# Sample heads as two planner streams ahead of the attention units, sparse keys prepared beside the last dense head

## The chip, the cores and the metric

One core of a Trainium2 chip. The time is device microseconds of one execution. The core has five engines that run their own instruction lists in order: TensorE (PE; its weight loads are shown as PEld), VectorE (DVE), ScalarE (ACT), GpSimd (POOL) and the sync engine (SP), which here issues all DMAs from one queue.

## What is computed

One layer of a hybrid attention encoder, for one new stream of 2048 frames (the prompt) and, beside it, 8 streams of 16 new frames each with 256 cached frames (the sample). One input projection feeds three groups of heads, and one output projection joins them:

```python
p = _split_proj(_rmsnorm(x, g), w_in, b_f)
oa = _forget_block(...)   # A: 8 heads, causal softmax attention with forget gates
ob = _dsa_block(...)      # B: 8 heads (2 of keys), attention over the best 256 keys of an indexer
oc = _band_prompt(...)    # C: 8 heads, own chunk and the 8 chunks before
y = x + concat(oa * silu(za), ob * silu(zb), oc * silu(zc)) @ w_out   # then RMSNorm
```

The sample goes through the same three kinds of heads (24 in all), with keys and values from the caches and from the new rows. Keys, values and queries are used as pairs of 16-bit halves, so every product is made of two or three matmuls.

## The kernel before

**A planner writes the order.** The kernel's Python is a set of generators, `Stream`s (line 163). Each yields a condition, a time by which its next inputs are due, and issues instructions when it is resumed. `drive` (line 436) keeps a clock of each engine by a table of costs (`Clock`, line 63) and resumes, again and again, the stream that is due: steps without TensorE go by their time, steps with TensorE go in the order in which the streams are handed to `drive`, the first that is due, and `slack` (line 48; 300 ns for the sample) holds a stream's matmuls back until their inputs are surely there. Gates (`gate`, `landed`, lines 423 to 430) open when something is planned to be done. All of it happens while the program is written: the engines see only their lists and semaphores. All instructions come from one helper, so the profile gives line 196 for all; they are told apart by their tiles.

**The stages.** After normalisation and gates, `load_stream` and `fill_stream` (lines 846, 855) run the input projection in groups of 256 columns (tiles `wt`, `hT`, `pj`, evacuated to `ev` and stored by DMA). The list `groups` (line 832) sets their sequence: pairs of A and C heads by `HO`, with five B groups between (keys and values, then four of queries and gates). The projection fills TensorE while the attention runs in `units` (`run`, line 1896): 16 dense heads (A and C) of 4 units each, then sparse blocks 15 down to 0 of 128 queries, 2 units each. A unit takes maxima of its scores (VectorE), scores (TensorE, tile `st`), exps (ScalarE, `Pf`), the low half (`Pl`, GpSimd or VectorE), and products (TensorE, `o`). `prep_stream` (line 1979) prepares each dense head: loads keys and values that the projection has stored (`kn`, `vn`), splits them (`khl`, `V`), turns the keys (`tr`, `Ka`, `K`). A head is prepared once the groups up to its own have landed. After the last dense head the same stream runs `b_prep`, the sparse heads' tables (`BTb`, `ng`) and keys and values (`KaB`, `VB`), when the projection is all done. `out_all` (line 1994) then runs the output projection (`wo`, `gac`) block by block; block 16, the sample's, opens when the sample is done.

**The sample** (`sample_stream`, line 1349; main loop from 1606) is one stream, started when the sparse selection is done. It has no memory of its own: it uses tiles that the selection leaves free. Loads of cached keys and values go to the halves of `rl`, split keys to `qi`, turned keys and the spread queries to `yy`, values and spread weights to `acc`, scores and weights to `cum`, bias to `eq`; its matmuls go through `pj`. Head after head, in this order: `keys`, bias, `softmax`, `products` of the head before, `values`. It stands behind the units in the list that is handed to `drive` (line 1941): select, load, products, rows, index scores, scores, maxima, preparation, sample, then the projection and the output projection as fillers.

Of the kernel before, what the change touches and what calls it, by code (L numbers as in the profile page):

```python
# [264 lines left out]
def hybrid_step(ctx, tc, x_prompt, x_sample, cache_a_k, cache_a_v, cache_a_logf, cache_b_k, cache_b_v,  # L265
# [1083 lines left out]
    def sample_stream():  # L1349
# [67 lines left out]

        def ahead(nm, src):

            def one(g0):  # L1420
                n = min(4, 17 - g0)
                t = row(nm)
                load(t, src, g0, n)
                return t

            nxt = [one(0), one(4)]
            for g0 in range(0, 17, 4):
                yield g0, min(4, 17 - g0), nxt.pop(0)
                if g0 + 8 < 17:
                    nxt.append(one(g0 + 8))  # L1430
# [175 lines left out]
        yield from gate_sums()  # L1606
        yield landed(grouped, last[sorder[0]])
        after = None
        order = [4 * g + r for g in sorder + [2, 3] for r in range(4)] + [0]
        for k, hg in enumerate(order[:-1]):  # L1610
            g, r = divmod(hg, 4)
            if hg == 8:
                if after is not None:
                    yield from after()
                    after = None
                yield from select_s()
                yield landed(grouped, last[2])
            if r == 0:
                qp4 = sl.tile([128, 4, 128], F16, name="qp4", bufs=1)
                q24 = sl.tile([128, 4, 128], F16, name="q24", bufs=1)  # L1620
                rows = [qTd[e, g * 256:(g + 1) * 256, SEQ:NT].rearrange("(h d) t -> d h t", d=64) for e in range(2)]
                SP.dma_start(qp4[0:64], rows[0])
                SP.dma_start(qp4[64:128], rows[0])
                SP.dma_start(q24[0:64], rows[1])
            if hg < 8:
                ks, vs, bias = parts(cak, sak, hg), parts(cav, sav, hg), gate_bias(hg)
            elif hg >= 16:
                ks, vs, bias = parts(cck, sck, hg - 16), parts(ccv, scv, hg - 16), rel_bias(hg - 8)
            else:
                ks, vs, bias = parts(cbk, sbk, g - 2), parts(cbv, sbv, g - 2), rel_bias(hg - 8)  # L1630
            new = hg < 8 or hg >= 16 or r == 0
            more, bias = bias, next(bias)
            if new:
                Ka = yield from keys(ks)
            yield from more
            hl = yield from softmax(qp4[:, r, :], q24[0:64, r, :], Ka, bias)
            if after is not None:
                yield from after()
                yield landed(grouped, last[order[k + 1] // 4])
            if r == 0:  # L1640
                SP.dma_start(sz4, szd[g * 4:(g + 1) * 4, 4, :, 0:64].rearrange("h p d -> p h d"))
            if new:
                yield from values(vs)

            def after(hl=hl, sz=sz4[:, r, :], gs=gs4, r=r, g=g):
                yield from products(*hl, sz, gs[:, r, :])
                if r == 3:
                    for e in range(2):
                        SP.dma_start(gTd[e, g * 256:(g + 1) * 256, SEQ:NT].rearrange("(h d) t -> d h t", d=64),
                                     gs[e * 64:(e + 1) * 64])  # L1650
        yield from after()
# [447 lines left out]
```

## Time and profile before

| | |
|---|---|
| median of 3 runs | 2649.38 us (2643.98 to 2650.48) |
| profiled execution | 2649.79 us, its span 2648.0 us |
| busy: PE / PEld | 2397.8 / 1674.7 us (91% / 63% of the span) |
| busy: DVE / ACT / POOL | 1802.8 / 1381.3 / 1100.3 us |
| DMA | 257.24 MB, mean 97 GB/s |
| mean granted TensorE clock | 0.973 of full speed |

The profile is one execution. The page cuts the span into 40 slices of 66.2 us and gives each engine's busy share in tenths; TensorE has 9 in nearly all of them, and less in the first, in four from 1655 us on (4, 7, 8, 8) and in the last (5). A waiting time is put down to what ended it. Busy time of TensorE is modelled, since matmuls overlap: the distance between the starts of two matmuls in a row says what one costs.

### The profile page before, as it was taken

The numbers are of one execution on the slowest core, as the hardware profiler recorded it, in microseconds if no ns is written. First come the engines' busy times: TensorE is split into PE (matmuls) and PEld (weight loads), VectorE is DVE, ScalarE is ACT, GpSimd is POOL, SyncE is SP. The second block draws the span as 40 slices with busy tenths as digits, with TensorE's granted clock in tenths as the row PEclk, the third lists the DMA queues.
The fourth block names the chain that finished last, engine by engine and source line by source line (L and its number), as shares of the span: only waits on it lengthen the run. The fifth ranks groups of instructions, "written<-read, shape, count | busy, mean of one in ns | idle before, by whom it ended". The sixth has DMA issues, their size and how long they took to land. (4 is left out here: it accounts for less than half of the span.)

```text
span 2648.0 us, 69046 instructions
## 1 busy us (share of the span) xinstructions
PE 2397.8 (91%) x26752; PEld 1674.7 (63%) x26838; DVE 1802.8 (68%) x4900; ACT 1381.3 (52%) x2734; POOL 1100.3 (42%) x1730
## 2 busy tenths in 40 slices
PE   4998999999999998999999999478899999999995
PEld 3666677766766776686776876355455555555543
DVE  6333778876787868778685566487866677778542
ACT  6324666766656774766744454365554444444110
POOL 0012556663443544534452043255665444544100
PEclk9999999999999999999999999689999999999997
DMA  6247323434343222233445433643533334334531
GB/s 192 60 92 198 92 67 80 107 96 99 94 94 106 71 76 76 72 103 83 120 99 124 120 76 81 135 94 67 144 83 86 79 83 106 84 86 108 127 99 26
DMA packets 553189, 257.24 MB, mean 97 GB/s; under 512 B 376064, under 2 KB 541760, under 8 KB 552592
## 3 DMA queue, kind: packets, MB, share of 16 engines
q1 hardware_dynamic: 552848, 252.71, 38.8%
q8 instruction: 212, 3.47, 0.6%
q14 instruction: 129, 1.06, 0.1%
HBM read 160.37 MB, written 84.85 MB: 93 GB/s over the span
## 5 line engine op out<-in xcount | busy, mean ns | idle before, releaser
L196 POOL TENSOR_TENSOR Pl<-Pf 128x512 f16<-128x512 f32 (+3 forms) x688 | 683.4, 1003 | 582.2 <-ACT Pf L196 544.6
L196 PE MATMUL pj<-wt,hT 128*128 128x128 f16 (+1 forms) x8568 | 779.2, 243 | 11.3 <-DVE ev L196 10.9
L196 PEld LDWEIGHTS <-hT 128*128 128x128 f16 x8976 | 653.2, 98 | 117.5 <-issue 22.0
L196 ACT ACTIVATE Pf<-st,sh 128x512 f32<-128x512 f32 (+1 forms) x496 | 297.9, 613 | 282.9 <-DVE st L196 111.1
L196 PEld LDWEIGHTS <-Pf 128*128 128x128 bf16 x5472 | 314.9, 98 | 104.2 <-issue 9.8
L196 PE MATMUL pj<-wo,gac 128*128 128x512 f16 x1224 | 290.5, 383 | 13.2 <-DMA gac<-gTd 11.6
L196 PE MATMUL pj<-hT,wt 128*128 128x512 f16 (+1 forms) x1440 | 293.6, 348 | 0.3 <-DVE ev L196 0.3
L196 PEld LDWEIGHTS <-Pl 128*128 128x128 f16 x2736 | 255.3, 99 | 18.5 <-POOL Pl L196 16.4
L196 DVE SCALAR_TENSOR_TENSOR acc<-rl,iws,acc 128x512 f32<-128x512 f32 (+3 forms) x266 | 196.2, 738 | 87.1 <-ACT rl L196 82.5
L196 DVE CUSTOM_DVE_ANT_0 jk<-s,ng 128x512 bf16<-128x512 f32 (+3 forms) x304 | 188.7, 621 | 84.6 <-PE s L196 67.4
L196 ACT ACTIVATE Pf<-st,ncb 128x512 f32<-128x512 f32 (+1 forms) x320 | 192.1, 623 | 92.8 <-PE st L196 80.3
L196 DVE TENSOR_REDUCE mx<-s 128x1 f32<-128x512 f32 (+2 forms) x320 | 185.0, 603 | 67.0 <-PE s L196 66.1
L196 ACT ACTIVATE rl<-s 128x512 f32<-128x512 f32 (+3 forms) x304 | 161.3, 544 | 110.8 <-PE s L196 55.7
L196 ACT ACTIVATE ev<-pj 128x512 f32<-128x512 f32 (+4 forms) x211 | 115.2, 546 | 194.0 <-PE pj L196 181.3
L196 PE MATMUL o<-V,Pf 128*128 128x65 f16 x3296 | 213.2, 194 | 1.0 <-ACT Pf L196 0.9
L196 PE MATMUL o<-V,Pl 128*128 128x65 f16 x1648 | 196.2, 193 | 13.3 <-POOL Pl L196 12.3
L196 PEld LDWEIGHTS <-wt 128*128 128x128 f16 x1440 | 126.3, 98 | 129.2 <-issue 13.9
L196 PEld LDWEIGHTS <-gac 128*128 128x128 f16 x1224 | 116.5, 98 | 139.5 <-DMA gac<-gTd 12.7
L196 PE MATMUL st<-qp,Ka 128*128 128x512 f16 (+3 forms) x544 | 180.9, 335 | 8.8 <-ACT Pf L196 8.7
L196 ACT ACTIVATE eq<-acc,us 128x384 bf16<-128x384 f32 (+13 forms) x126 | 165.4, 1313 | 39.6 <-POOL us L196 38.0
L196 PE MATMUL st<-Q,K 98*128 98x512 f16 (+3 forms) x544 | 182.2, 336 | 1.7 <-ACT Q L196 1.7
L196 PE MATMUL o<-VB,Pf 128*128 128x65 f16 (+1 forms) x2176 | 132.4, 194 | 3.6 <-DVE rq_t L196 1.9
(449 smaller groups left out, 4299.8 us busy)
## 6 DMA issues: line engine op xcount, KB each, us to landing
wst<-in_w_in SPq DMA_DIRECT2D x84, 256.0 KB
gac<-gTd SPq DMA_DIRECT2D x34, 384.0 KB
out<-ev SPq DMA_DIRECT2D x96, 128.0 KB
qTd<-ev SPq DMA_DIRECT2D x96, 128.0 KB
szd<-ev SPq DMA_DIRECT2D x96, 128.0 KB
qp<-qTd SPq DMA_DIRECT2D x96, 128.0 KB
out<-xr SPq DMA_DIRECT2D x17, 512.0 KB
xt<-in_x_prompt SPq DMA_DIRECT2D x16, 512.0 KB
```

Of the source, the lines that this page charges most:

```text
L196: r = f(*args, **kw)
```

## The change

Three things change; the arithmetic stays.

1. The last group of the projection is now the fourth group of B queries and gates, which only the sparse heads read. It stood before the last pairs of A heads. The marks that sparse heads wait for (`last[2]`, `last[3]`) move with it.
2. `b_prep` leaves `prep_stream` and becomes a stream of its own, with the same gate (projection done).
3. The sample becomes two streams. `first` makes keys, bias, scores and weights of head after head, `second` values, products and the output. Plain lists join them: `first` is at most one head ahead of `second`; `begin` asks for the first two tiles of the next head's keys or values as soon as the ones before are used. Both stand ahead of the units in the list for `drive`.

```diff
-        if 2 <= k < 7:
+        if 2 <= k < 6:
             groups += [(group_b, max(k - 3, 0), int(k > 2))]
-            last[2] = last[3] = len(groups)
...
+    groups += [(group_b, 3, 1)]
+    last[2] = last[3] = len(groups)
...
+        early = {}
         def ahead(nm, src):
...
-            nxt = [one(0), one(4)]
+            nxt = early.pop(nm, None) or [one(nm, src, 0), one(nm, src, 4)]
...
+        def begin(nm, src):
+            early[nm] = [one(nm, src, 0), one(nm, src, 4)]
...
+        def first():
+            yield from gate_sums()
+            yield upto(order[0])
+            for k, hg in enumerate(order):
+                g, r = divmod(hg, 4)
+                if hg == 8:
+                    yield gate(lambda: len(done) == k)
+                    yield from select_s()
...
+                bias = gate_bias(hg) if hg < 8 else rel_bias(hg - 8)
+                more, bias = bias, next(bias)
+                if fresh(hg):
+                    Ka = yield from keys(stored(hg)[0])
+                yield from more
+                yield gate(lambda: len(done) >= k - 1)
+                weights.append((yield from softmax(qp4[:, r, :], q24[0:64, r, :], Ka, bias)))
+                if k + 1 < len(order):
+                    yield upto(order[k + 1])
+                    if fresh(order[k + 1]) and order[k + 1] != 8:
+                        begin("kn", stored(order[k + 1])[0])
+        def second():
+            yield upto(order[0])
+            begin("vn", stored(order[0])[1])
+            for k, hg in enumerate(order):
+                g, r = divmod(hg, 4)
+                if fresh(hg):
+                    yield from values(stored(hg)[1])
...
+                if k + 1 < len(order) and fresh(order[k + 1]):
+                    yield upto(order[k + 1])
+                    begin("vn", stored(order[k + 1])[1])
+                yield gate(lambda: len(weights) > k)
+                yield from products(*weights[k], sz4[:, r, :], gs4[:, r, :])
+                done.append(k)
...
-        drive(*others[:2], Stream(products()), Stream(rows()), *others[2:3], Stream(scores()), Stream(maxima(), 400.0), *others[3:], *fillers)
+        drive(*others[:4], Stream(products()), Stream(rows()), *others[4:5], Stream(scores()), Stream(maxima(), 400.0), *others[5:], *fillers)
...
-        yield gate(lambda: not fill_s.live)
-        yield from b_prep()
-        aw_done.append(1)
+        prepared.append(1)
+    def sparse_prep_stream():
+        yield gate(lambda: not fill_s.live)
+        yield from b_prep()
+        prepared.append(1)
...
-    run(units + b_units, lambda u: True, [Stream(select_stream(), 0.0), load_s, Stream(score_stream()), Stream(prep_stream(), 300.0),
-                                          smp_s], [fill_s, Stream(out_all())])
+    run(units + b_units, lambda u: True, [Stream(select_stream(), 0.0), load_s, smp_s, smp2_s, Stream(score_stream()), Stream(prep_stream(), 300.0),
+                                          Stream(sparse_prep_stream(), 300.0)], [fill_s, Stream(out_all())])
```

What this makes of the order is seen at two places. The first is ScalarE's list where the keys of the second to last dense head are split (`khl<-kn`, with the values `V<-vn`). `ev<-pj` evacuates the projection, `acc<-rl` and `qi<-rl` are the sample's values and keys, `yy<-pj` its turned keys, `gh<-u` the end of a unit. Before:

```order
L196 ACTIVATE ev<-pj 128x128
L196 ACTIVATE gh<-u 128x4x64
L196 ACTIVATE acc<-rl 128x4x64 x2
L196 ACTIVATE acc<-rl 128x64
L196 ACTIVATE qi<-rl 128x4x64
L196 ACTIVATE yy<-pj 128x512
L196 ACTIVATE qi<-rl 128x4x64
L196 ACTIVATE khl<-kn 128x4x64
L196 ACTIVATE V_2320<-vn 128x4x64
```

and now:

```order
L196 ACTIVATE khl<-kn 128x4x64
L196 ACTIVATE V_2320<-vn 128x4x64
L196 ACTIVATE ev<-pj 128x512
L196 ACTIVATE acc<-rl 128x4x64 x2
L196 ACTIVATE Ka<-tr 128x512
L196 ACTIVATE khl<-kn 128x4x64
L196 ACTIVATE V_2320<-vn 128x4x64
L196 ACTIVATE yy<-pj 128x512
L196 ACTIVATE Ka<-tr 128x512
L196 ACTIVATE ev<-pj 128x512
```

Before, the last evacuation of the projection stands ahead of the first split of these keys. Now evacuations stand between the splits, with the sample's loaded values and keys among them in both cases.

The second is VectorE's list behind the last sparse block: `rs<-o`, `u<-o,rs` and `gh<-u,gh` end the block, `acc<-pj`, `srs`, `cum<-pj,srs` and `acc<-cum,acc` are products of a sample head, `xr`, `ms` and `rq` belong to the output projection. Before:

```order
L196 RECIPROCAL rs<-o 128x4
L196 TENSOR_TENSOR u<-o,rs 128x256
L196 COPY acc<-pj 128x2x8x16 x2
L196 COPY acc<-pj 128x128 x2
L196 TENSOR_TENSOR gh<-u,gh 128x256
L196 RECIPROCAL srs<-pj 128x1
L196 TENSOR_SCALAR cum<-pj,srs 128x64
L196 TENSOR_TENSOR acc<-cum,acc 128x64
L196 SCALAR_TENSOR_TENSOR xr<-pj,xr 128x512
L196 TENSOR_TENSOR ms<-ss 128x1
```

and now:

```order
L196 RECIPROCAL rs<-o 128x4
L196 TENSOR_TENSOR u<-o,rs 128x256
L196 TENSOR_TENSOR gh<-u,gh 128x256
L196 SCALAR_TENSOR_TENSOR xr<-pj,xr 128x512
L196 TENSOR_TENSOR ms<-ss 128x1
L196 TENSOR_SCALAR ms<-ms 128x1
L196 TENSOR_SCALAR rq_i<-ms 128x1
L196 TENSOR_SCALAR rq_h<-ms 128x1
L196 TENSOR_SCALAR rq_i<-rq_i 128x1
L196 TENSOR_TENSOR rq_t<-rq_i 128x1
```

The sample's rows are gone from here. Every later row of VectorE's list is one of the output projection too; before, six more passes of the sample's scores and eight of its products stood behind the last sparse block.

## Rows read from the trace of the kernel before

**Rows 1.** Busy time by stretch. First column: the stretch, in us from the start of the span; then its length; busy us of each engine with its number of instructions (PE is TensorE, PEld its weight loads, DVE VectorE, ACT ScalarE, POOL GpSimd); the clock that TensorE was granted, as a share of full speed; the DMA engines' busy share; GB/s.

```profile
1437.60:1663.40 225.80, 218.38 (x2832) 167.64 (x2829) 124.94 (x311) 106.65 (x229) 70.48 (x84) 0.98 0.39 92
...
1663.40:1972.40 309.00, 236.06 (x2801) 149.96 (x2819) 223.01 (x558) 163.49 (x319) 154.13 (x158) 0.89 0.44 106
...
1675.00:1725.00 50.00, 24.82 (x201) 16.18 (x202) 24.55 (x70) 19.20 (x47) 7.75 (x10) 0.60 0.72 161
...
1725.00:1925.00 200.00, 162.66 (x2009) 103.02 (x2018) 165.95 (x393) 119.36 (x226) 116.73 (x117) 0.94 0.40 100
...
1972.40:2471.60 499.20, 476.48 (x4942) 283.53 (x5005) 369.80 (x1157) 224.18 (x431) 240.34 (x244) 0.99 0.41 94
...
2575.00:2648.00 73.00, 37.77 (x330) 22.38 (x330) 18.29 (x75) 3.70 (x10) 3.95 (x8) 0.73 0.13 33
```

**Rows 2.** All engines in order of time, where the projection ends (from 1663.9 us). Columns: start us, duration us, engine, line, operation, output<-input, number; in brackets the idle time before it and what ended it. SPq is the sync engine's DMA queue; its duration is the time the queue needed for that issue.

```profile
1664.33 4.52 SPq L196 DMA_DIRECT2D szd<-ev  x2
...
1664.48 1.51 PE L196 MATMUL pj<-wt,hT 128*128 128x128 f16 x24
...
1669.92 0.94 SPq L196 DMA_DIRECT2D rl<-in_cache_a_v  x2
...
1672.42 0.90 ACT L196 ACTIVATE acc<-rl 128x256 f16<-128x256 f32 x2 [5.80 <-DMA rl<-in_cache_a_v]
...
1676.21 0.61 PE L196 MATMUL pj<-idh,qi 128*128 128x128 f16 x4 [10.21 <-DVE qi L196]
...
1677.36 0.50 SPq L196 DMA_DIRECT2D BTb<-rep  x1
...
1677.65 0.41 ACT L196 ACTIVATE khl<-kn 128x256 f16<-128x256 f32 x1
```

**Rows 3.** The views of two tiles, the sparse heads' keys (KaB) and values (VB): durations in ns (shortest, median, longest), then the first and the last start in us.

```profile
L196 PE MATMUL s<-KaB,qp x320: 216/377/634, 1832.5 to 2455.2; 128*128 128x512 f16 x136, 128*128 128x384 f16 x8, 128*128 128x256 f16 x8, 128*128 128x128 f16 x8
...
L196 PE MATMUL o<-VB,Pl x1088: 191/192/247, 1856.0 to 2471.7; 128*128 128x65 f16 x182
```

**Rows 4.** TensorE in order of time, 1640 to 1663 us: pairs of rows, a run of matmuls and the row that follows it, so that the difference of the starts is what the run took.

```profile
1641.94 1.46 PE L196 MATMUL pj<-hT,wt 128*128 128x512 f16 x6
...
1643.24 0.22 PE L196 MATMUL o<-V,Pf 128*128 128x65 f16 x2
...
1650.73 0.27 PE L196 MATMUL pj<-yy,acc 128*128 128x256 f16 x1
...
1652.79 0.24 PE L196 MATMUL o<-V,Pf 128*128 128x65 f16 x2
...
1656.57 0.33 PE L196 MATMUL pj<-idb,cum 128*128 128x128 bf16 x3
...
1656.90 0.33 PE L196 MATMUL st<-qp,Ka 128*128 128x384 f16 x1
...
1658.63 1.70 PE L196 MATMUL pj<-acc 128*128 128x65 f16 x51
...
1660.17 0.22 PE L196 MATMUL o<-V,Pf 128*128 128x65 f16 x2
...
1661.17 1.83 PE L196 MATMUL pj<-wt,hT 128*128 128x128 f16 x30
...
1662.84 0.83 PE L196 MATMUL pj<-hT,wt 128*128 128x128 f16 x12
```

**Rows 5.** VectorE by operation and shape, from 2475 to 2610 us, where GpSimd has next to nothing to do. Columns: count, busy us, mean ns of one, idle us before.

```profile
L196 DVE SCALAR_TENSOR_TENSOR qi<-rl,qi 128x256 f16<-128x256 f32 x4 | 1.7, 423 | 4.9 <-ACT qi L196 4.9
...
L196 DVE SCALAR_TENSOR_TENSOR acc<-rl,acc 128x256 f16<-128x256 f32 x4 | 1.7, 418 | 0.0
...
L196 DVE CUSTOM_DVE_ANT_0 cum<-pj,eq 128x384 f32<-128x384 f32 x6 | 3.3, 556 | 8.0 <-PE pj L196 4.1 <-issue 3.9
...
L196 DVE TENSOR_TENSOR cum<-cum 128x384 f16<-128x384 f32 x3 | 1.7, 552 | 0.7 <-ACT cum L196 0.7
...
L196 DVE COPY acc<-pj 128x256 bf16<-128x256 bf16 x7 | 2.0, 285 | 1.6 <-PE pj L196 1.6
```

**Rows 6.** The same view from 1725 to 1925 us, where GpSimd is busy 117 of 200 us.

```profile
L196 DVE SCALAR_TENSOR_TENSOR acc<-rl,acc 128x256 f16<-128x256 f32 x13 | 7.9, 607 | 2.5 <-ACT acc L196 2.4
...
L196 DVE SCALAR_TENSOR_TENSOR qi<-rl,qi 128x256 f16<-128x256 f32 x14 | 7.4, 529 | 2.8 <-ACT qi L196 2.7
```

**Rows 7.** TensorE by operation, from 2471.6 us to the end.

```profile
L196 PE MATMUL pj<-wo,gac 128*128 128x512 f16 x456 | 104.0, 386 | 12.6 <-DMA gac<-gTd 11.6 <-DVE xr L196 1.0
```

**Rows 8.** The chain of work that ended last, its end: start us, us, what.

```profile
2617.65 17.61 PE pj L196 x70
...
2635.28 0.70 DVE xr L196
```

**Rows 9.** Waits of TensorE's weight loads for what the sample prepares: in the whole run for the split keys (tile qi) and for the spread weights and values (tile acc), total us and times; then the same two by the view of the waits, from 1650 to 1725 and from 2575 us, total us, times, longest.

```profile
  PEld L196: 36.1, 20
...
  PEld L196: 23.2, 18
...
PEld L196 <- DVE qi L196: 24.5, 5, 10.4
...
PEld L196 <- DVE acc L196: 12.8, 6, 3.4
```

**Rows 10.** GpSimd by operation and shape, from 1725 to 1925 us.

```profile
L196 POOL TENSOR_TENSOR Pl<-Pf 128x512 f16<-128x512 f32 x77 | 85.6, 1127 | 62.6 <-ACT Pf L196 61.9
```

More of the change, by code (lines that the diff above doesn't have):

```diff
@@ L1346, in bias, with sample @@
             G.memset(CN[0:64, 576:640], NEG)
-    def sample_stream():
+    def sample():
         def big(nm, bufs, dt=F16):
@@ L1604, in select_s @@
             V.tensor_scalar(nsel, nsel, NEG, None, op0=ALU.mult)
[L1606 to L1624, printed above, removed]
-            if hg < 8:
[L1626 to L1646, printed above, removed]
@@ new lines, in stored, with fresh, upto @@
+        def stored(hg):
+            if hg < 8:
+                return parts(cak, sak, hg), parts(cav, sav, hg)
+            if hg >= 16:
+                return parts(cck, sck, hg - 16), parts(ccv, scv, hg - 16)
+            return parts(cbk, sbk, hg // 4 - 2), parts(cbv, sbv, hg // 4 - 2)
+        def fresh(hg):
+            return hg < 8 or hg >= 16 or hg % 4 == 0
+        order = [4 * g + r for g in sorder + [2, 3] for r in range(4)]
+        weights, done = [], []
+        def upto(hg):
+            return landed(grouped, last[hg // 4])
@@ new lines, in first @@
+        def first():
[6 more added lines that the diff above has]
+                    yield from select_s()
+                if r == 0:
+                    qp4 = sl.tile([128, 4, 128], F16, name="qp4", bufs=1)
+                    q24 = sl.tile([128, 4, 128], F16, name="q24", bufs=1)
+                    rows = [qTd[e, g * 256:(g + 1) * 256, SEQ:NT].rearrange("(h d) t -> d h t", d=64) for e in range(2)]
+                    SP.dma_start(qp4[0:64], rows[0])
+                    SP.dma_start(qp4[64:128], rows[0])
+                    SP.dma_start(q24[0:64], rows[1])
+                bias = gate_bias(hg) if hg < 8 else rel_bias(hg - 8)
[9 more added lines that the diff above has]
+                        begin("kn", stored(order[k + 1])[0])
@@ L1649, in after @@
                         SP.dma_start(gTd[e, g * 256:(g + 1) * 256, SEQ:NT].rearrange("(h d) t -> d h t", d=64),
-                                     gs[e * 64:(e + 1) * 64])
-        yield from after()
+                                     gs4[e * 64:(e + 1) * 64])
+        return first(), second()
     sorder = sorted([0, 1, 4, 5], key=lambda g: last[g])
@@ L1983, in prep_stream, with smp2_stream @@
             yield from h.prep()
+        prepared.append(1)
+    def sparse_prep_stream():
         yield gate(lambda: not fill_s.live)
         yield from b_prep()
-        aw_done.append(1)
-    aw_done = []
+        prepared.append(1)
+    prepared = []
+    halves = []
     def smp_stream():
         yield gate(lambda: state["selected"] == 14)
-        yield from sample_stream()
+        halves.extend(sample())
+        yield from halves[0]
+    def smp2_stream():
+        yield gate(lambda: halves)
+        yield from halves[1]
     def out_all():
-        yield gate(lambda: len(ended) >= na and aw_done)
+        yield gate(lambda: len(ended) >= na and len(prepared) == 2)
         aw_end.close()
```

17 lines of the change are left out of this document (9 added, 8 removed).

## The prediction

> **What bounds the kernel now.** I read the busy time by stretch first, then the order of time in the gaps, then the durations of what the change moves. In the stretch by stretch view [rows 1] TensorE works 218.4 of 225.8 us while projection groups are still there to fill it (1437.6 to 1663.4), and 476.5 of 499.2 us among the sparse blocks (1972.4 to 2471.6): there TensorE is the bound, and about 0.97 of the time is the most it reaches. Two places are different. From 1663.4 to 1972.4 it is busy 236.1 of 309.0 us at a mean granted clock of 0.89; VectorE, at 223.0, is nearly as full. From 2575 to the end it is busy 37.8 of 73.0 us at 0.73. Those two places are what the change works on; before 1437.6 it moves little.
>
> What happens at 1664 is seen in order of time [rows 2]. The last projection matmuls start at 1664.48. The sync queue stands 4.52 us at a store of the projection's results, so the sample's value loads behind it are issued only at 1669.92; ScalarE waits 5.80 us for them, and behind that instruction stand its splits of the keys; TensorE gets its next matmul at 1676.21, after 10.21 us of nothing. The keys of the last two dense heads are first split at 1677.65, and the sparse heads' tables are asked for at 1677.36. From 1675 to 1725 TensorE is busy 24.8 us of 50, at a mean clock of 0.60 [rows 1], most of it at the lower level (1.2 GHz of 2.4) after those 10 us of standing: 24.8 x 0.60 is 15 us of work at full clock, 35 us are lost, and with the 9 us between the last projection matmul and 1675 the hole costs 44 us. The first matmul with the sparse keys starts at 1832.5, the last sparse product at 2471.7 [rows 3].
>
> **The change, part by part.**
>
> *The projection group that only the sparse heads need goes last.* The last pair of dense heads then has its own groups one earlier, and is prepared beside that group instead of after it. The group is 96 matmuls of 512 columns at 0.217 us (six from 1641.94 to 1643.24) and 24 + 408 of 128 columns at 0.056 us (thirty from 1661.17 to 1662.84) [rows 4]: 20.8 + 24.2 = 45 us. That is as long as the hole. The work is the same; it now lies where TensorE stood. Its evacuations and stores go with it: the orders above show them between the keys of the last heads.
>
> *Sparse preparation as a stream of its own.* It starts when the group is done, while the units of the second to last head run, and no longer waits for the preparation of the last dense head. Its two copies of tables and the K/V loads keep their number and their queue. It adds nothing and I give it nothing of its own: what hides it is the units of the last head and a half; without that cover it is a wait for tables and keys, inside the 44 us that a rival below prices.
>
> *The sample as two streams.* No instruction goes away. Per head TensorE has 17 transposes of keys (17 x 0.056 = 0.9), the scores from 1650.73 to 1652.79 (2.1), six transposes of weights from 1656.57 to 1656.90 (0.3) and 51 products from 1658.63 to 1660.17 (1.5) [rows 4]: 4.9 us. VectorE has five splits of keys and five of values at 0.42 us with nobody beside them (the fifth is short: 9 x 0.42 = 3.8), bias with maximum and the low half 0.55 each, four copies at up to 0.285, and half a dozen small ones below that [rows 5]: 7.5 us. In the order, between the last dense unit before the hole and the end of sparse block 14, five passes of sample scores stood before and nine stand now: four heads more in the crowded stretch. None is left behind the last sparse block, where the order of before has six passes of scores and eight of products.
>
> *The crowded stretch.* It now holds 45 + 4 x 4.9 = 65 us more of TensorE. Of its 236.1 us busy time 10 us in the hole (24.8 against 15) and about 10 us from 1725 to 1925 (162.7 at 0.94) are slow clock, so its work is 216 us; with the 65 it is 281, which at 0.97 takes 290 us. VectorE gets 4 x 7.5 = 30 us more. In the crowd the splits took 0.607 and 0.529 us, 0.15 more than alone [rows 5, 6]: nine a head, four heads, 6 us. 223 + 36 = 259 us. From 1725 to 1925, the longest piece in which VectorE was the fuller engine, it did 165.95 of 200 us, 0.83 [rows 1]. 259 / 0.83 = 312 us. I take this, the longer of the two: the stretch stays about as long as it is, but holds 65 us more, which elsewhere took 65 / 0.97 = 67 us. **Gain 309 + 67 - 312 = 64 us.** GpSimd is busy 154 of 309 us there and gets three short operations a head; it is not the bound.
>
> On those splits the Trainium skill speaks against the change: its page "SBUF — State Buffer", section "Who interferes with whom", has a VectorE instruction with two SBUF inputs and a GpSimd instruction that reads SBUF exclude each other for a whole instruction. The rows agree that such splits are slower beside GpSimd, but by 0.15 us on the mean and not by a whole GpSimd instruction. What a full exclusion would give is the second rival.
>
> *The tail.* From the last sparse product to the end are 2648.0 - 2471.7 = 176 us. By the order 456 matmuls of the output projection and the sample pieces stand there, now 378 and no sample. The 456 took 104.0 us [rows 7], 0.228 each: 378 x 0.228 = 86 us. Behind the last matmul, started in the run of 17.61 us from 2617.65, VectorE's first step is at 2635.28, and the normalisation and the store take the 12.7 us to the end [rows 8]; that stays. 99 us instead of 176. What left, 78 x 0.217 = 17 us and 28 us of the sample (6 x 2.1, 8 x 1.85, one head's keys), must be done earlier: 45 / 0.97 = 47 us, if TensorE is the bound there. **Gain 176 - 99 - 47 = 30 us.**
>
> *The price of being first.* The planner now puts a sample step ahead of the units' products. Its gates stand in the planner, so no engine stands at them; but an engine stands at any sample instruction whose data is later than planned, with the units' instructions queued behind. TensorE's weight loads waited 36.1 us for split keys and 23.2 us for the sample's spread weights in the whole run; 24.5 of the first lie in the hole and 12.8 of the second after 2575 [rows 9]. The other 22 us are about 0.9 us for each of 24 heads. Such a wait costs nothing more if loads come earlier (the first two tiles of the next head are now asked for as soon as the one before is done, and pass the stores in the sync queue), or up to 5.80 us a head if each meets a wait like the one at 1672 [rows 2]. Every head's steps lie closer together; nearest is the 0.9, so I add a third of it again: **8 us** lost.
>
> **Sum**, against the profiled execution, 2649.79 us for a span of 2648.0: 2649.8 - 64 - 30 + 8 = **2564 us**. That execution is 0.4 us above the median of the runs shown (2649.38). A measurement of this kernel can tell about 0.3%, 8 us, from no change.
>
> **The rivals.**
>
> *VectorE sets the stretch more than I think.* Over the whole 309 us its share was only 0.72 (223.0 of 309.0 [rows 1]), since it waits for scores, and its waits may stay. 259 / 0.72 = 360 us instead of 312: 2564 + 48 = **2612 us**. For it: VectorE never passed 0.83 for long; against it: the 0.72 has the hole in it, where it did 24.55 of 50. By the page's rule, with each of 40 splits waiting out a GpSimd subtraction of 1.127 us [rows 10], it would be 40 x 0.98 / 0.83 = 47 us, nearly the same time, 2611; the means of the splits [rows 5, 6] are against the rule in this strength. Chance 0.16 for the two.
>
> *The hole stays.* The last heads' loads could still come late, since the tables and the group's own stores share the queue. Then the stretch is 312 + 44 us: **2608 us**. For it: the queue's 4.52 us at a store [rows 2]. Against: the order has the splits of the keys among the group's evacuations. Chance 0.07. Both rivals together give 2656 us, no change: 0.04.
>
> *Slower.* One mechanism: sample loads behind stores in the sync queue, ScalarE in order behind the load, exps and TensorE in order behind ScalarE, as at 1664 to 1676, but now once in every head, because the sample goes first. 24 heads at 4.4 us beyond what I price are 106 us: **2670 us**. It decides from (2657.4 - 2564) / 24 = 3.9 us a head. For it is the one wait of 10.21 us; against it, the mean of 0.9 us outside the hole, and that projection and output matmuls lie between. Chance 0.06.
>
> *Better still.* If TensorE sets the stretch (290 us) and the sample costs no new waits, 2649.8 - 86 - 30 = **2534 us**; part of the forecast's range, with 0.03 for less than that.
>
> **How the numbers follow.** The forecast has 0.64. The range goes from just below the clean case, 2530, to just above the two single rivals, 2618 us. Faster by over 0.3%: 0.64 + 0.16 + 0.07 + 0.03 = 0.90; within 0.3% 0.04; slower 0.06.
>
> **What would show it.** Right: TensorE busy over 0.9 in the 60 us behind the point where the last dense heads' keys are split, granted clock near 1 there; the last sparse product later than now by less than 20 us or earlier, at most 102 us before the end; only output projection behind it; VectorE the fuller engine from the last dense head to sparse block 14. Wrong: a gap of 10 us at a sample transpose with ScalarE behind a load; splits of the sample over 1 us; units waiting for ScalarE throughout while the sample runs; a tail still over 120 us.

## The result, and the profile after

The median is 2606.52 us (2603.13 to 2610.06, 4 runs) against 2647.8 (2643.98 to 2650.48): ratio 0.9851, 95% interval 0.9834 to 0.9868, so 41 us less where 86 were forecast. The profiled execution is the fastest of the four, 2603.13 us, its span 2601.3.

The view of busy time by stretch, kernel after, cut at the ends of units as [rows 1] is: the two units where the hole was, the next two, units 60 to 63, sparse blocks 15 and 14, blocks 13 to 0, and the tail; the last two rows look closer at the second stretch.

```profile
1614.60:1684.00 69.40, 68.32 (x900) 51.91 (x900) 41.39 (x120) 34.41 (x85) 10.95 (x16) 1.00 0.51 125
1684.00:1757.40 73.40, 51.64 (x680) 35.30 (x677) 45.89 (x116) 35.16 (x76) 36.08 (x37) 0.84 0.56 137
1757.40:1821.50 64.10, 53.79 (x748) 36.40 (x746) 52.01 (x128) 38.85 (x86) 41.32 (x47) 0.97 0.34 77
1821.50:1961.40 139.90, 122.82 (x1377) 72.64 (x1374) 101.16 (x273) 76.88 (x139) 67.32 (x68) 0.93 0.44 115
1961.40:2506.80 545.40, 514.93 (x5332) 303.60 (x5328) 379.39 (x1222) 216.11 (x407) 247.03 (x254) 0.98 0.35 84
2506.80:2601.30 94.50, 81.77 (x385) 36.93 (x381) 35.46 (x146) 8.37 (x23) 0.72 (x1) 0.95 0.39 102
1700.00:1725.00 25.00, 12.42 (x176) 7.96 (x173) 12.64 (x29) 6.83 (x16) 9.61 (x10) 0.80 0.85 204
1725.00:1750.00 25.00, 18.40 (x204) 12.06 (x204) 16.16 (x39) 15.44 (x34) 13.48 (x13) 0.79 0.42 104
```

The old hole is filled: TensorE works 68.32 of 69.40 us at full clock. Behind it a new one opens at 1700. The tile views that answer to [rows 3], and TensorE behind the last sparse product, as [rows 7]:

```profile
L196 PE MATMUL s<-KaB,qp x320: 216/377/634, 1804.6 to 2494.5; 128*128 128x512 f16 x136, 128*128 128x384 f16 x8, 128*128 128x256 f16 x8, 128*128 128x128 f16 x8
L196 PE MATMUL o<-VB,Pl x1088: 191/192/247, 1835.8 to 2506.8; 128*128 128x65 f16 x182
...
L196 PE MATMUL pj<-wo,gac 128*128 128x512 f16 x378 | 81.7, 379 | 0.0
```

The sparse keys are used 28 us earlier, but the last sparse product is 35 us later; behind it stands output projection alone. The new hole in order of time, the sync queue, ScalarE and TensorE apart (columns as in [rows 2]):

```profile
1698.80 0.37 SPq L196 DMA_DIRECT2D rl<-in_cache_c_k  x1
...
1700.32 2.97 SPq L196 DMA_DIRECT2D qp<-qTd  x2
...
1713.29 0.61 SPq L196 DMA_DIRECT2D Q2b<-qTd  x1
...
1722.31 0.53 SPq L196 DMA_DIRECT2D rl<-in_cache_c_v  x1
```

```profile
1718.97 0.42 ACT L196 ACTIVATE qi<-rl 128x256 f16<-128x256 f32 x1 [7.52 <-DMA rl<-in_cache_c_k]
1719.42 0.59 ACT L196 ACTIVATE Q<-tr 2x512 f16<-2x512 f32 x1
1727.14 0.42 ACT L196 ACTIVATE acc<-rl 128x256 f16<-128x256 f32 x1 [7.14 <-DMA rl<-in_cache_c_v]
```

```profile
1713.44 0.38 PE L196 MATMUL st<-qp,Ka 128*128 128x512 f16 x1
1720.06 0.58 PE L196 MATMUL st<-Q,K 98*128 98x512 f16 x1 [6.24 <-ACT Q L196]
1720.44 0.63 PE L196 MATMUL st<-qp,Ka 128*128 128x512 f16 x1
...
1728.33 0.58 PE L196 MATMUL st<-qp,Ka 128*128 128x512 f16 x1 [6.67 <-ACT Pf L196]
```

The queries of the first sparse blocks (qp, Q2b) are issued in a row from 1700 to 1714, ahead of the sample's next cache loads; from 1700 to 1725 the DMA engines are 0.85 busy. ScalarE stands 7.52 and 7.14 us at a sample load; the row of the units (Q) and their exps (Pf) are queued behind, and TensorE stands 6.24 and 6.67 us, then works at the lower clock (a matmul of 512 columns 0.63 us instead of 0.38).

### The profile page after: what moved, and what is told of

Same layout as the page of the kernel before. It is cut to its first block, busy times and chain, and to the rows that moved or that the text cites. A ratio compares the mean times of both kernels' runs of the same rounds, so it can differ in the third digit from the quotient of the medians.

```text
span 2601.3 us, 69167 instructions
## 1 busy us (share of the span) xinstructions
PE 2391.1 (92%) x26838; PEld 1665.9 (64%) x26838; DVE 1797.3 (69%) x4905; ACT 1374.4 (53%) x2734; POOL 1092.9 (42%) x1725
## 5 line engine op out<-in xcount | busy, mean ns | idle before, releaser
L196 POOL TENSOR_TENSOR Pl<-Pf 128x512 f16<-128x512 f32 (+3 forms) x683 | 675.1, 999 | 680.1 <-ACT Pf L196 643.8
L196 PE MATMUL pj<-wo,gac 128*128 128x512 f16 x1224 | 283.9, 379 | 0.0
```

The source lines that it names most:

```text
L196: r = f(*args, **kw)
```

## The experiments

Four theories. **1**: the hole moved; late sample loads make it. **2**: VectorE bounds the stretch. **3**: being first costs the units more than 8 us. **4**, formed after the first four runs: where the sample is one stream, its own chain sets the end. All ratios, with 95% intervals, are to runs of the kernel before that were made beside each version (their medians lie between 2647.8 and 2651.9 us), so a difference of a few us between two versions is not sure. The "stretch" is from the last product of unit 55 to that of sparse block 14, 346.8 us in after.

**The parts apart.** The group's order alone:

```diff
-        if 2 <= k < 7:
+        if 2 <= k < 6:
...
+    groups += [(group_b, 3, 1)]
+    last[2] = last[3] = len(groups)
```

> The kernel before with the order of the projection groups alone changed (the last q/z group of the sparse heads comes at the end of the list); sample and sparse preparation stay as they were. Theory 1 (the hole at the start of the sparse part only moved: when the projection ends, the loads for the sparse heads and the sample's cache loads share the DMA engines, ScalarE stands in order on a late one and TensorE behind it): the 44 us hole is filled with 45 us of projection, but 20 to 30 us of waiting come back right behind it, so 2620 to 2635 us. Theory 2 (VectorE bounds the stretch, because the sample's denser VectorE work now lies in it): without the new place of the sample nothing comes back, 2600 to 2610 us.

Measured: 2660.47 us, 1.0042 (1.0027 to 1.0058), slower. Both theories missed.

The sample's two streams ahead of the units, alone (diff: that of the change without the two other parts).

> The kernel after with the groups' order and the sparse preparation put back, so that the two sample streams ahead of the units are the only change against before. The forecast's terms for the sample were 30 us less in the tail and 8 us for being first. Theory 1: the hole of 44 us is there as before and the sample stands in it as the units do, the tail's gain is seen nearly whole, 2620 to 2635 us. Theory 2: VectorE is the bound of the stretch from the hole to sparse block 14, which gets 35 us longer with the sample's work, so the tail's gain is eaten there, 2645 to 2660 us.

Measured: 2622.16 us, 0.9902 (0.987 to 0.9935): 27 us won, in theory 1's range and near the forecast's two terms for the sample (30 - 8).

Everything but the sample (here and below the diff shows what the paragraph speaks of; this one is to the kernel before, with the group's order as above):

```diff
-                                          smp_s], [fill_s, Stream(out_all())])
+                                          Stream(sparse_prep_stream(), 300.0), smp_s], [fill_s, Stream(out_all())])
```

> The kernel after with the sample as it was before (one stream, behind the units); the order of the groups and the separate sparse preparation stay. Theory 1: as with the order of the groups alone, a part of the hole comes back when the projection ends, 2610 to 2630 us, and ScalarE waits for a sample cache load of more than 5 us are seen between 1680 and 1760 us. Theory 2: the crowded stretch has less VectorE work in it and no wait of that kind; the hole's 44 us are won whole, 2600 to 2608 us, and the tail stays at some 176 us.

Measured: 2660.82 us, 1.0047 (1.0031 to 1.0063); again both missed. Here are its stretch, blocks 13 to 0 and tail, and the first of TensorE's waits in that tail (total us, times, longest):

```profile
1599.60:1914.40 314.80, 272.74 (x3351) 179.16 (x3348) 230.43 (x557) 167.04 (x325) 156.43 (x159) 0.92 0.45 111
1914.40:2404.90 490.50, 477.28 (x5067) 280.90 (x5064) 357.55 (x1135) 222.07 (x429) 239.78 (x246) 1.00 0.42 94
2404.90:2653.40 248.50, 169.66 (x1200) 95.36 (x1195) 95.90 (x355) 36.44 (x95) 13.88 (x25) 0.82 0.28 68
```

```profile
PE pj L196 <- DVE acc L196: 43.7, 16, 11.3
```

The last sparse product ends 67 us earlier than before. But the sample, one head after another behind the units, ends at 2612 us as it did before at 2605, and TensorE waits for its spread weights. The three rows leave TensorE 134 us without work. The same stretches of before leave about 128: by its rows also 134 (308.9 + 499.2 + 176.4 us, 850.7 busy), but its trace lacks 86 records of the matmuls that add the masks (26752 matmuls to 26838 weight loads), an estimated 6 us of busy time by what leaving out as many takes off in after. So nothing of the hole is won in all; it went to the tail. Theory 4 comes from this.

Two streams, but behind the units (diff to the kernel after):

```diff
-        drive(*others[:4], Stream(products()), Stream(rows()), *others[4:5], Stream(scores()), Stream(maxima(), 400.0), *others[5:], *fillers)
+        drive(*others[:2], Stream(products()), Stream(rows()), *others[2:3], Stream(scores()), Stream(maxima(), 400.0), *others[3:], *fillers)
...
-                                          Stream(sparse_prep_stream(), 300.0)], [fill_s, Stream(out_all())])
+                                          Stream(sparse_prep_stream(), 300.0), smp_s, smp2_s], [fill_s, Stream(out_all())])
```

> The kernel after with the two sample streams placed behind the units and the preparations instead of ahead of them; all else as in the kernel after. Theory 1 (the waits come from loads, not from the place in the list): the stretch from 1615 us to the end of sparse block 14 is still 340 us or more; the sample ends later and a part of the tail comes back, 2605 to 2630 us. Theory 3 (being first costs the units 9 to 17 us in the sparse blocks and more in the crowded stretch): 2580 to 2600 us if the sample still ends before the last sparse block.

Measured: 2576.93 us, 0.9722 (0.969 to 0.9754), 30 us better than the change, and better than any theory had it. By the same three pieces, in an execution that is the slowest of its four (2584.35 us):

```profile
1609.60:1965.00 355.40, 305.72 (x3748) 204.07 (x3745) 258.26 (x653) 189.39 (x392) 154.64 (x165) 0.92 0.48 114
1965.00:2442.80 477.80, 466.75 (x5206) 285.38 (x5203) 365.00 (x1153) 213.44 (x401) 241.51 (x253) 0.99 0.37 85
2442.80:2582.60 139.80, 127.02 (x592) 57.40 (x588) 52.78 (x218) 12.59 (x35) 0.72 (x1) 0.97 0.39 106
```

Theory 1 is right that the stretch does not depend on the place (355 us), theory 3 that the sparse blocks do: TensorE is without work for 11 us there, in after for 30.5. The tail is longer but full of output matmuls, 127 of 139.8 us. The two that complete the squares are the kernel without the sample's change with its one stream moved ahead, and the kernel before with both streams behind and nothing else:

```diff
-        drive(*others[:2], Stream(products()), Stream(rows()), *others[2:3], Stream(scores()), Stream(maxima(), 400.0), *others[3:], *fillers)
+        drive(*others[:3], Stream(products()), Stream(rows()), *others[3:4], Stream(scores()), Stream(maxima(), 400.0), *others[4:], *fillers)
```

> The fourth of two by two: the sample as one stream, as before, but ahead of the units; groups and sparse preparation as after. (One stream behind: 2661 us, two behind: 2577, two ahead: 2606.) Theory 4 (with one stream behind the units the sample's own chain sets the end; the end is the later of that chain and of TensorE's work, and whatever gets the chain through before the last sparse block wins the hole's 44 us): ahead of the units one stream gets through earlier than behind, though later than two, the sample ends at 2400 to 2480 us and the whole takes 2595 to 2625 us. If the place in the list does nothing for a chain that waits for itself, the sample still ends after 2550 us and the whole takes 2640 us or more.

Measured: 2622.76 us, 0.9893 (0.9869 to 0.9917). The time is in theory 4's range, the sample's end is not: it comes at 2581 us instead of 2612, where 2400 to 2480 was expected, still well behind the last sparse product (2449.5). So the place alone does not get a chain that waits for itself through in time.

> The kernel before with the sample as two streams behind the units, and nothing else changed: the projection groups and the sparse preparation stay as before, so the hole is there. Against the 2577 us of the same with the hole filled this gives what filling the hole is worth when the sample no longer sets the end. By the forecast's terms 44 us of hole and up to 64 with what follows: 2620 to 2640 us. If the hole's filling is mostly given back in the crowded stretch whatever the sample does: 2585 to 2605 us.

Measured: 2615.94 us, 0.9866 (0.9844 to 0.9887), between the two. Against 2577: the filled hole is worth 39 us with both streams behind. With both ahead it is worth 16, and with one stream behind, where the sample sets the end, less than nothing.

| sample | hole as before | hole filled |
|---|---|---|
| one stream, behind | 2649 | 2661 |
| one stream, ahead | - | 2623 |
| two streams, behind | 2616 | 2577 |
| two streams, ahead | 2622 | 2606 |

**The loads.** A one-column memset on POOL holds the first sparse loads at their place in the program (likewise for two masks and the first gates):

```diff
+                            if i >= 12:
+                                nc.gpsimd.memset(qp[:, 0, 0:1], 0.0)
+                                nc.gpsimd.memset(st["Q2"][2 * (c2 % 2) + gg][0:64, 0, 0:1], 0.0)
...
+                        if i >= 14:
+                            nc.gpsimd.memset(ng[:, 0:1], 0.0)
                         SP.dma_start(ng, negd[i])
```

> The kernel after, with the first loads of the sparse heads' queries, of the first two selection masks and of the first two gates held back: a one-column memset on POOL, at the place in the order where the loads stand in the program, has to come first. Instruction order of the engines is otherwise as after. In after these loads come at 1700 to 1724 us, ahead of the sample's cache loads in the sync queue. Theory 1 (late sample loads, ScalarE standing in order behind them, make the new hole of units 58 and 59): ScalarE's waits of 7.5 and 7.1 us for the sample's cache go, units 58 and 59 take 58 to 62 us instead of 73, the whole 2590 to 2598 us against 2606. Theory 2 (VectorE bounds the stretch): VectorE has the same work, 2603 to 2609 us.

Measured: 2597.79 us, 0.9818 (0.9795 to 0.9841), in theory 1's range. Units 58 and 59, 64.9 us instead of 73.4, and what ScalarE waited there for the sample's loads:

```profile
1683.30:1748.20 64.90, 51.62 (x676) 35.75 (x673) 45.97 (x116) 35.14 (x76) 36.61 (x37) 0.87 0.44 110
...
L196 ACT ACTIVATE qi<-rl 128x256 f16<-128x256 f32 (+1 forms) x8 | 3.1, 393 | 0.4 <-DMA rl<-in_cache_c_k 0.4
...
L196 ACT ACTIVATE acc<-rl 128x256 f16<-128x256 f32 (+1 forms) x6 | 2.3, 386 | 2.9 <-DMA rl<-in_cache_c_v 2.9
```

> The kernel after without the sample's cache loads that stand between the end of the projection and the end of the sparse keys' preparation (the sample's heads of that stretch run on stale rows); the order of every computing engine is word for word that of after. Theory 1: no sample load can be late there, units 58 and 59 take 58 to 62 us, the whole 2588 to 2596 us; this is the most that any repair of the loads could win. Theory 2: 2602 to 2609 us.

```diff
-                    SP.dma_start(dst[:, a - g0:b - g0, :], ap[:, a - j0:b - j0, :])
+                    e = SP0 if stretch() else SP
+                    e.dma_start(dst[:, a - g0:b - g0, :], ap[:, a - j0:b - j0, :])
```

(SP0 moves the planner's clock and issues nothing.)

Measured: 2597.46 us, 0.9792 (0.9771 to 0.9813), between the two ranges; units 58 and 59 took 63.8 us. In these two units the waits go or shrink and the units get shorter, so theory 1's mechanism is shown, but its size is 8.5 to 9.6 us, not the 11 to 15 I gave it. Holding wins about what leaving out wins. In the whole time it is at the edge of what can be told: the interval of the held loads overlaps that of the change (0.9834 to 0.9868) a little. The same step in a second kernel bears it out:

> The same held loads in the kernel with the two sample streams behind the units (2577 us). Theory 1: ScalarE's waits of 5.8 and 5.7 us for the sample's cache go, 2563 to 2571 us. Theory 2: nothing, 2574 to 2580 us.

Measured: 2566.45 us, 0.9686 (0.967 to 0.9702): in theory 1's range, and the best of all versions.

**VectorE.** The sample's splits twice (the values' split likewise), and in the other kernel not at all, from unit 56 to sparse block 14:

```diff
                 split_lo(khl[:, :n, 1, :], kn[:, :n, :], QS, khl[:, :n, 0, :])
+                if 56 <= ndone[0] < 68:
+                    nc.vector.scalar_tensor_tensor(khl[:, :n, 1, :], kn[:, :n, :], QS, khl[:, :n, 0, :], op0=ALU.mult, op1=ALU.subtract)
```

> The kernel after with each of the sample's key and value splits on VectorE issued twice from the end of unit 55 to the end of sparse block 14 (84 more instructions of about 0.42 us, 35 us of VectorE work into a stretch of 347 us, of which VectorE is busy 240); the order is otherwise that of after. Theory 2 (VectorE bounds the stretch): most of the 35 us is seen, 2625 to 2641 us. Theory 1 (it has slack, the stretch loses its time to waits for loads): 2606 to 2615 us.

> The kernel after without the sample's key and value splits on VectorE from the end of unit 55 to the end of sparse block 14 (the low halves there are those of an earlier head): the 35 us of work that were doubled in the run before are taken away; the order is otherwise that of after. Theory 2: VectorE bounds the stretch in this direction too, 2572 to 2590 us. Theory 1: the stretch waits for loads, 2600 to 2606 us. Between them, if VectorE bounds only a part of the stretch: 2590 to 2600 us.

The two stretches:

```profile
1617.70:1991.60 373.90, 302.41 (x3692) 197.67 (x3689) 287.52 (x719) 187.42 (x383) 158.77 (x167) 0.91 0.42 106
```

```profile
1617.10:1951.60 334.50, 288.66 (x3672) 195.60 (x3690) 210.91 (x557) 185.16 (x383) 154.79 (x167) 0.94 0.49 118
```

Doubled: 2634.28 us, 0.995 (0.9932 to 0.9967), in theory 2's range; VectorE is busy 47 us more than in after, the stretch 27 us longer. Without: 2596.85 us, 0.9808 (0.9785 to 0.9831), in the range between the theories; 30 us less, 12 us shorter. So a microsecond added costs 0.58 us of stretch, one taken away gives 0.42. The second figure holds more than VectorE's work: without the splits VectorE's waits in front of them are gone, too.

The third edit on VectorE's work takes the units' maxima over half of the columns:

```diff
+    def mxr(o, i):
+        if 56 <= ndone[0] < 68:
+            VN.reduce_max(o, i, axis=AX.X)
+            nc.vector.reduce_max(o, i[:, ::2], axis=AX.X)
+        else:
+            V.reduce_max(o, i, axis=AX.X)
...
-                    V.reduce_max(mx[:, ii, kc:kc + 1], p[:, :w], axis=AX.X)
+                    mxr(mx[:, ii, kc:kc + 1], p[:, :w])
```

(VN moves the planner's clock alone; the maxima of the sparse blocks, made by another instruction, are changed likewise.)

> The kernel after with the units' maxima on VectorE taken over every second column only from the end of unit 55 to the end of sparse block 14 (the shift of the softmax is then that of half of the keys); some 120 instructions of 0.69 us get about 0.25 to 0.3 us shorter, 30 to 36 us of VectorE work less on the units' own path; the order is that of after. Theory 2 in its strict form (VectorE holds the stretch on the units' path, where TensorE waited 13 us for maxima): the stretch gets 20 us or more shorter, 2575 to 2588 us. If the stretch is a chain through several engines, of which none is full: as with the splits, 2590 to 2600 us.

Measured: 2602.14 us, 0.9812 (0.9796 to 0.9829): VectorE is busy 27 us less, the stretch is 343.3 us, 3.5 less than after. The time is a little above the second range; theory 2 in its strict form is out. The last of these joins this edit with the two that leave out loads and splits:

> The three together on the kernel after: no sample cache loads between the end of the projection and the end of the sparse preparation, no sample splits on VectorE, and maxima over every second column, the last two from unit 56 to sparse block 14. If late loads and VectorE's work are the whole of the 35 us missed: the stretch comes to 300 to 315 us, the whole to 2560 to 2575 us. If a third cause is left (the sample's work on TensorE, ScalarE or POOL): the stretch stays above 322 us, the whole above 2580 us.

Measured: 2577.47 us, 0.972 (0.9704 to 0.9736).

```profile
1619.50:1935.90 316.40, 288.85 (x3692) 195.97 (x3689) 177.58 (x557) 184.73 (x383) 156.32 (x167) 0.95 0.49 118
```

The stretch is 316 us, 30 less than after; it and the time lie between the two ranges. That it is close to the 312 forecast does not prove the forecast's sum: VectorE has 63 us less work here than in after and 45 less than in before, and by the forecast's own rule (the longer of VectorE's work at 0.83 and TensorE's 290) the stretch would be 290. So late loads and VectorE's work matter, but something else holds the stretch as well. Whether the three give more together than alone is not settled: by the stretch they give 30.4 against 9.6 + 12.3 + 3.5 us, by the ratios 35 against 37.

**Attempts at more.** All three with held loads.

> The kernel with two streams behind the units and the held sparse loads (2566 us), and the splitting of the output weights begun after sparse block 14 instead of after the last dense unit: 12 VectorE instructions of 1.44 us (17.3 us) and as many copies on ScalarE leave the stretch for the sparse blocks 13 to 11, where VectorE is busy 0.75 of the time and TensorE 0.97. Theory 2: the stretch gets 12 to 17 us shorter and the sparse blocks hardly longer, 2550 to 2560 us. Theory 1: 2564 to 2570 us. A cost that could eat it: the output matmuls of blocks 15 and 14 come later and are missing as filling in the stretch's gaps; then no change.

```diff
-        yield gate(lambda: len(ended) >= na and len(prepared) == 2)
+        yield gate(lambda: len(ended) >= na + 4 and len(prepared) == 2)
```

Measured: 2580.99 us, 0.9737 (0.9717 to 0.9757), 15 us worse than 2566 and outside every range. Stretch and tail of the 2566 us, then of this:

```profile
1600.70:1946.30 345.60, 301.13 (x3750) 201.50 (x3747) 256.40 (x653) 188.81 (x392) 156.32 (x177) 0.94 0.48 117
...
2423.90:2563.80 139.90, 127.07 (x594) 57.36 (x590) 52.82 (x218) 12.58 (x35) 0.72 (x1) 0.96 0.39 107
```

```profile
1609.90:1941.20 331.30, 289.41 (x3706) 197.91 (x3723) 242.87 (x655) 177.40 (x380) 153.59 (x178) 0.94 0.43 103
...
2403.70:2580.40 176.70, 163.86 (x811) 75.13 (x807) 66.40 (x275) 16.15 (x46) 1.05 (x2) 0.97 0.40 107
```

The stretch is 14 us shorter, as theory 2 has it, but 30 output matmuls (7.3 us) have left it, too, so this does not tell the theories apart. The output matmuls that had filled gaps come back behind the last product: 36.8 us more tail.

> The kernel with two streams behind the units and the held sparse loads (2566 us), and both sample streams stopped between the end of the projection and the end of the sparse keys' preparation. Theory 2: the sample's VectorE work (some 15 to 25 us) leaves units 58 to 63, which get 10 to 20 us shorter; the sample, which ended 30 us before the last sparse product, ends some 60 us later, beside output matmuls, 2545 to 2562 us. If work is only moved (the stretch loses time that the sparse blocks or the tail give back): 2563 to 2575 us.

```diff
+    def held_back(steps):
+        for w in steps:
+            yield w
+            if not fill_s.live and not b_units[0].open_():
+                yield gate(b_units[0].open_)
...
-        yield from halves[0]
+        yield from held_back(halves[0])
```

Measured: 2586.18 us, 0.9761 (0.9745 to 0.9777), worse than both ranges. Units 58 and 59 fall from 65.7 to 48.3 us and the stretch from 345.6 to 337.7, but blocks 13 to 0 grow from 477.6 to 498.6: the whole loses 20.

> The kernel after with the held sparse loads and with the first stream (keys to weights) behind the units, the second (values to products) ahead of them. Both ahead: 2598 us, both behind: 2566 us. Theory 3 (what costs is VectorE work of the sample let in ahead of the units' maxima): the first stream has the longer VectorE chain (split, masks, maxima, weights), so most of the 31 us is won, 2566 to 2580 us. If the products' 51 matmuls in one piece ahead of the units' are what costs: 2585 to 2600 us.

```diff
-load_s, smp_s, smp2_s, Stream(score_stream()), Stream(prep_stream(), 300.0),
-                                          Stream(sparse_prep_stream(), 300.0)], [fill_s, Stream(out_all())])
+load_s, smp2_s, Stream(score_stream()), Stream(prep_stream(), 300.0),
+                                          Stream(sparse_prep_stream(), 300.0), smp_s], [fill_s, Stream(out_all())])
```

Measured: 2576.45 us, 0.9725 (0.9706 to 0.9745): two thirds of the difference between both ahead and both behind belong to the first stream's place. That is theory 3's range; that it is VectorE's work which costs, and not the stream's matmuls, this run does not show.

## Why the prediction was half right

| piece | before | forecast | after |
|---|---|---|---|
| up to unit 55 | 1663.5 | -46 (group of 45 us moved out) | -48.9 |
| stretch | 309 | +3 (312) | +37.9 (346.8) |
| blocks 13 to 0 | 499.2 | -21 + 47 + 8 = +34 | +46.2 (545.4) |
| tail | 176.4 | -77 (99) | -81.9 (94.5) |
| sum | | -86 | -46.7 |

- **The group and the hole: right.** It fills the two units at 0.98, clock 1.00 (forecast: over 0.9).
- **The tail: right**, 94.5 us, 378 matmuls in 81.7 us, nothing of the sample.
- **Two signs of "right" failed.** The last sparse product came 35 us later (less than 20 was the sign), and VectorE was not the fuller engine of the stretch (240 us against TensorE's 297).
- **The crowded stretch: the step that failed**, 35 of the 39 us missed. The prediction let VectorE set its length: 259 us of work at a share of 0.83, which I read from the one piece of before where VectorE had been fullest. The work was less, 240 us, but the share was 0.69, and in no kernel here above 0.77 (the doubled splits, 287.52 of 373.90). VectorE alone did not set the length, or 27 us less of its work on the units' path would have given more than 3.5. The whole stretch of after, and the four largest of TensorE's waits in it (total us, times, longest):

```profile
1614.60:1961.40 346.80, 296.57 (x3688) 196.25 (x3688) 240.45 (x637) 185.29 (x383) 155.67 (x167) 0.93 0.46 115
```

```profile
PE s L196 <- DVE mx L196: 13.5, 31, 1.5
PE st L196 <- ACT Pf L196: 8.5, 5, 6.7
PE tr L196 <- DVE mh L196: 7.6, 5, 2.7
PE st L196 <- ACT Q L196: 6.6, 2, 6.2
```

TensorE stands 50 us: 21 for VectorE's maxima and rows of the units (mx, mh), 15 for ScalarE, 13 of them at the two late loads, the rest in small pieces, most of them for the sample's tiles. And about 21 of its 296.6 busy us are the lower clock (296.6 x 0.07, the way the prediction worked it out for before), where the forecast counted its 281 us at full clock. This reads as a chain through several engines, none of them full. By experiment, 9 of the 35 us are the late sample loads; how the other 26 split between VectorE's work, the sample's waits and the clock stays open.

- **The rivals.** The first gives nearly the measured time, 2612 us by the share of 0.72. Part of that is luck: its 360 us are 259 us of work at 0.72, where 240 at 0.69 were measured, and its cause, VectorE alone, is not borne out. The stated range, too, holds the measured time only because it was drawn out to the two single rivals. The waits of the fourth (a late sample load, ScalarE in order behind it) stop TensorE for over 6 us twice, not in every head.
- **The price of being first: too small.** Blocks 13 to 0 took 12 us more than forecast. Against the run with both streams behind, TensorE stands 19.5 us longer there (30.5 - 11), instead of 8 (by its own working, a third of 22, it would have been 7.3). Against before itself it is about 12 (30.5 against 22.7, of which an estimated 4 are the records that its trace lacks), so a part of these 12 us of the miss is busy time and not standing. (35 + 12, less 3 and 5 gained in the first and last rows, are 39.)
- **What the sum did not say:** its terms hang together. I had put 44 to 64 us on the hole whatever the sample did. With the sample as it was, filling it was worth -12 us, because the sample's chain set the end; in the change itself it was worth 16 (2622 to 2606).

The splits took 0.548 and 0.480 us in the stretch (after, 1684 to 1961), 0.06 to 0.13 more than alone [rows 5]:

```profile
L196 DVE SCALAR_TENSOR_TENSOR qi<-rl,qi 128x256 f16<-128x256 f32 x25 | 13.7, 548 | 6.9 <-ACT qi L196 6.9
L196 DVE SCALAR_TENSOR_TENSOR acc<-rl,acc 128x256 f16<-128x256 f32 x24 | 11.5, 480 | 9.3 <-ACT acc L196 9.3
```

The Trainium skill's page "SBUF — State Buffer", section "Who interferes with whom", would have each wait out a GpSimd instruction that reads SBUF and came first. The trace agrees, split by split; the prediction, which read the means alone, missed it. Taken one by one, 35 of these 49 splits start with no two-input GpSimd instruction (TENSOR_TENSOR, mostly the subtractions Pl<-Pf) under way and take 0.42 us on the mean, 0.43 at most. Five of them start under a GpSimd memset, which only writes, and are as fast. The other 14 start with such an instruction under way; each ends 0.28 us after it and takes up to 1.26 us, but for one, which had 0.08 us left to wait and takes 0.42. Two pairs, GpSimd's row and then VectorE's:

```profile
1892.12 1.04 POOL L196 TENSOR_TENSOR Pl<-Pf 128x512 f16<-128x512 f32 x1 [0.24 <-ACT Pf L196]
...
1892.34 1.10 DVE L196 SCALAR_TENSOR_TENSOR qi<-rl,qi 128x256 f16<-128x256 f32 x1
...
1933.30 1.04 POOL L196 TENSOR_TENSOR Pl<-Pf 128x512 f16<-128x512 f32 x1 [0.81 <-ACT Pf L196]
...
1933.57 1.06 DVE L196 SCALAR_TENSOR_TENSOR acc<-rl,acc 128x256 f16<-128x256 f32 x1 [1.56 <-ACT acc L196]
```

What the second rival had wrong is how often: it let every split meet a GpSimd subtraction and wait 0.98 us. Together the 14 took some 5 us longer than 0.42 us each, where it put 47.

## What to carry to other kernels

Before a gap is filled, ask which chain sets the end: with 44 us of gap filled and the chain left as it was, the time went up by 12 us. A share of an engine that held for 200 us of one stretch is not its share when more work comes in; the mean over the whole stretch, gap and all (0.72), was the better guide here, where a new gap took the old one's place. A mean duration can hide two cases: most splits were as fast as alone, and a few waited. And a chain that only has to be done by the end was better put behind the work that bounds the time, as two overlapping streams, than ahead of it (2577 against 2606 us).

## What the runs showed of the hardware

- A maximum on VectorE over every second column of PSUM took as long as one over as many neighbouring ones: 256 of 512 columns in the run with half maxima, then 256 in a row in after (count, busy us, mean ns):

```profile
L1189 DVE TENSOR_REDUCE mx<-s 128x1 f32<-128x256 f32 x56 | 22.4, 416 | 8.3 <-PE s L196 7.7
```

```profile
L196 DVE TENSOR_REDUCE mx<-s 128x1 f32<-128x256 f32 x8 | 3.3, 415 | 0.2 <-PE s L196 0.2
```

- Transfers issued early are not free: with the sparse queries, masks and gates held back, the same bytes later, ScalarE's longest wait for a sample load in units 58 and 59 fell from 7.5 to 2.9 us.
- TensorE came out of waits of 6.24 and 6.67 us at the lower of its two clocks (1.2 GHz of 2.4), and the two halves of the 50 us from 1700 had 0.80 and 0.79 of full speed on the mean.
